# A rotary-embedding kernel: the two batches of a paired transfer lie 12 MB apart in DRAM instead of 2 MB

## Chip, cores and metric

The kernel runs on one core of a Trainium2 chip. The metric is the time of one execution in device microseconds (us), with the median over several executions.

## The reference

`x` has 16 batches of 512 positions with 1024 numbers each, read as 16 heads of 64. Each head is cut into halves `x1` and `x2`, which are rotated by tables that depend on the position alone:

```python
cos = cos[None, :, None, :]
sin = sin[None, :, None, :]
rotated = np.concatenate([x1 * cos - x2 * sin, x1 * sin + x2 * cos], axis=-1)
```

Input and output are 33.55 MB each. Every number is read once and written once, with two products and one sum on it.

## The kernel before

Batches 0, 1, 14 and 15 travel alone, as 128 partitions with 4 positions (16 KB) each. Batches 2 to 13 travel in pairs: 64 row groups of 8 positions (32 KB) from each of two batches, so that partition 2s belongs to the first batch of the pair and partition 2s + 1 to the second. A tile of `x` lands in a ring of 40 rows in on-chip memory, is worked on in place and is stored from there.

```python
singles = (0, 1, batch - 2, batch - 1)
tiles = [(b, R1 if b in singles else R2) for b in range(batch) if b in singles or b % 2 == 0]
RING = 5 * R2
...
x2 = x.rearrange("b (s r) d -> s b (r d)", r=R2)
...
def in_dram(single, pairs, t):
    b, n = tiles[t]
    return single[b] if n == R1 else pairs[:, b:b + 2, :]
...
def on_sync(sp):                       # all loads
    for t, (b, n) in enumerate(tiles):
        if b * R1 % R2 == 0 and b * R1 >= RING:
            k = (b * R1 - RING) // R2
            sp.wait_ge(sem_out[k], 16 * stores_of(k))      # ring slot free
        sp.dma_start(in_sbuf(t), in_dram(x1, x2, t)).then_inc(sem_in[t], 16)
...
ae.dma_start(in_dram(o1, o2, t), in_sbuf(t))               # the stores, from ScalarE's queue
```

Per row, GpSimd (POOL) forms the product with `sin` (58 of the 64 rows; VectorE forms it for one row of each pair tile), VectorE (DVE) the product with `cos`, and the sum is made by VectorE or, for 21 of the 64 rows, by TensorE (PE) with ScalarE (ACT) copying it back.

## Time and profile before

| | before |
|---|---|
| time, median of 3 | 161.3 us (161.3 to 161.43) |
| the profiled execution, and its span | 167.47 us, 166.1 us: slow state |
| DMA engines busy, loads + stores | 48.3% + 47.3% of 16 engines |
| POOL, DVE, PE busy | 82%, 79%, 44% |
| moved | 67.26 MB |

The span is the time from the first to the last instruction. The share of the DMA queues is the time that their packets took, against 16 engines over the whole span, so two queues that add up to nearly 100% leave hardly any moment in which an engine has nothing to move.

### The profile page before, as it was taken

What the parts mean: (1) busy time and instruction counts of PE and PEld (TensorE: products, weight loads), DVE (VectorE), ACT (ScalarE), POOL (GpSimd) and SP (SyncE); (2) the same over time, 40 slices, a digit from 0 to 9 for tenths busy, and PEclk for the clock granted to TensorE, in tenths of its full rate; (3) what the DMA queues carried; (4) which work ended last, traced back from release to release, by engine and by line L of the source; (5) the groups of instructions that cost most, each with busy time, mean ns of one, the idle gap of its engine ahead of it and who ended that gap; (6) DMA issues with size and microseconds to landing.
All of it is one profiled execution on the core that took longest, in us unless ns stands there. A gap on an engine that the chain in (4) does not pass through costs nothing.

```text
span 166.1 us, 568 instructions
## 1 busy us (share of the span) xinstructions
PE 72.6 (44%) x94; PEld 24.6 (15%) x94; DVE 130.5 (79%) x117; ACT 24.0 (14%) x26; POOL 136.6 (82%) x67
## 2 busy tenths in 40 slices
PE   6040006196629371924292909381193827800000
PEld 1020002041202011301130213020130212200000
DVE  0069997798999999999999899972999997069600
ACT  3020000204022201222022011302022022110000
POOL 5059999999999999999999799962999999069500
PEclk9999999957696975599659555955559555595555
DMA  5999999999999999999989999999999999999293
GB/s 158 427 425 458 450 391 426 462 391 418 446 489 387 444 434 403 482 363 412 466 387 482 395 403 466 395 442 426 403 478 426 387 422 458 442 395 434 107 383 142
DMA packets 3170, 67.26 MB, mean 405 GB/s; under 512 B 352, under 2 KB 608, under 8 KB 608
## 3 DMA queue, kind: packets, MB, share of 16 engines
q1 hardware_dynamic: 1728, 33.69, 48.3%
q10 hardware_dynamic: 1440, 33.56, 47.3%
q14 instruction: 2, 0.02, 0.0%
HBM read 33.69 MB, written 33.55 MB: 405 GB/s over the span
## 4 chain that ended last, share of the span: by engine, by line
DMA 52%; POOL 15%; issue 11%; DVE 8%; PE 6%; ACT 1%; SPq 1%; POOLq 0%; DVEq 0%; ACTq 0%
DMA x_sb<-in_x_dram 33%; DMA out_dram<-x_sb 19%; POOL t_sb L254 15%; PE t_ps L209 6%; DVE x_sb L301 4%; DVE t_ps L290 4%; ACT x_sb L175 1%; SPq L156 1%; SPq L159 1%; DVE t_sb L283 0%; DVEq L300 0%; POOLq L145 0%; POOLq L143 0%; ACTq L136 0%
## 5 line engine op out<-in xcount | busy, mean ns | idle before, releaser
L254 POOL TENSOR_TENSOR t_sb<-x_sb,s_sb 128x1024 f32<-128x1024 f32 x58 | 134.2, 2355 | 18.7 <-DMA x_sb<-in_x_dram 11.7
L209 PE MATMUL t_ps<-t_sb,ident 128*128 128x512 f32 x84 | 67.8, 966 | 65.3 <-POOL t_sb L254 45.1
L290 DVE TENSOR_TENSOR t_ps<-x_sb,pair_ps 128x1024 f32<-128x1024 f32 x48 | 57.9, 1222 | 8.1 <-DMA x_sb<-in_x_dram 4.8
L301 DVE TENSOR_TENSOR x_sb<-t_ps,t_sb 128x1024 f32<-128x1024 f32 x43 | 52.4, 1220 | 2.7 <-POOL t_sb L254 2.5
L209 PEld LDWEIGHTS t_ps<-t_sb,ident 128*128 128x128 f32 x84 | 22.7, 295 | 109.6 <-issue 62.1
L175 ACT ACTIVATE x_sb<-t_ps 128x1024 f32<-128x1024 f32 x21 | 21.5, 1024 | 112.0 <-PE t_ps L209 112.0
L290 DVE TENSOR_TENSOR t_ps<-x_sb,tab_ps 128x1024 f32<-128x1024 f32 x16 | 19.3, 1222 | 7.1 <-DMA x_sb<-in_x_dram 6.7
L283 DVE TENSOR_TENSOR t_sb<-x_sb,tab_ps 128x1024 f32<-128x1024 f32 x6 | 7.3, 1215 | 0.0
L261 DVE COPY tab_ps<-stage 128x128 f32<-128x128 f32 x1 | 0.3, 295 | 8.1 <-DMA stage<-in_cos_dram 8.1
L192 PE MATMUL pair_ps<-stage,pick 128*128 128x256 f32 x4 | 2.0, 664 | 5.6 <-DMA stage<-in_sin_dram 5.6
L185 PE MATMUL t_ps<-zero 128*128 128x512 bf16 x6 | 2.7, 630 | 1.3 <-DVE zero L259 1.3
L192 PEld LDWEIGHTS pair_ps<-stage,pick 128*128 128x128 f32 x4 | 1.2, 322 | 6.6 <-issue 6.4
L235 POOL TENSOR_SCALAR_AFFINE_SELECT pick<-pick 128x128 f32<-128x128 f32 x2 | 1.4, 706 | 0.1
L165 ACT ACT_TABLE_LOAD x1 | 1.3, 1283 | 0.8 <-PEq L334 0.8
L165 ACT ACTIVATE s_sb<-stage 128x128 f32<-128x128 f32 x1 | 0.3, 309 | 7.4 <-DMA stage<-in_sin_dram 7.4
L185 PEld LDWEIGHTS t_ps<-zero 128*128 128x128 bf16 x6 | 0.7, 137 | 2.4 <-DVE zero L259 1.2
L259 DVE MEMSET zero<- 128x256 uint32 x1 | 0.3, 272 | 0.9 <-PEq L334 0.9
L169 ACT ACTIVATE s_sb<-pair_ps 128x256 f32<-128x256 f32 x1 | 0.4, 384 | 1.7 <-PE pair_ps L192 1.7
L220 POOL MEMSET ident<- 128x128 f32 x1 | 0.2, 205 | 0.3 <-POOLq L334 0.3
L170 ACT ACTIVATE s_sb<-pair_ps 128x256 f32<-128x256 f32 x1 | 0.4, 377 | 0.0
L222 POOL TENSOR_SCALAR_AFFINE_SELECT ident<-ident 128x128 f32<-128x128 f32 x1 | 0.3, 297 | 0.1
L334 POOL MEMSET const-float32-0.0<- 128x1 f32 x1 | 0.1, 99 | 0.3 <-issue 0.3
(7 smaller groups left out, 1.3 us busy)
## 6 DMA issues: line engine op xcount, KB each, us to landing
x_sb<-in_x_dram SPq DMA_DIRECT2D x6, 4096.0 KB, 39.3
out_dram<-x_sb ACTq DMA_DIRECT2D x6, 4096.0 KB, 30.4
x_sb<-in_x_dram SPq DMA_DIRECT2D x4, 2048.0 KB, 24.3
out_dram<-x_sb ACTq DMA_DIRECT2D x4, 2048.0 KB, 17.6
stage<-in_cos_dram SPq DMA_DIRECT2D x1, 64.0 KB, 8.0
stage<-in_sin_dram SPq DMA_DIRECT2D x1, 64.0 KB, 7.7
```

The lines of the kernel that those rows point to most:

```text
L156: sp.dma_start(in_sbuf(t), in_dram(x1, x2, t)).then_inc(sem_in[t], 16)
L159: sp.dma_start(stage[:, i, :], table.rearrange("(s r) d -> s (r d)", r=R1)).then_inc(sem, 16)
L165: ae.activation(s1_sb[:, :, 0, :], sv, COPY, scale=-1.0)
L175: ae.activation(xs[:, k, :], t1_ps[:, u % NT1, :], COPY).then_inc(sem_a, 1)
L185: pe.matmul(t1_ps[:, k, b * BANK:(b + 1) * BANK], zero[:, 0:P], zero[:], start=True, stop=True).then_inc(sem_w, 1)
L192: pe.matmul(pair_ps[:, k].rearrange("p c r d -> p (c r d)"), pick[:, k].rearrange("q s b -> q (s b)"), stage[:].rearrange("q c f -> q (c f)"),
L209: ins = pe.matmul(t1_ps[:, u % NT1, b * BANK:(b + 1) * BANK], ident[:], t2[:, b * BANK:(b + 1) * BANK], start=False, stop=True, skip_group ...
L235: pl.affine_select(out=pick[:, k], in_=pick[:, k], compare_op=mybir.AluOpType.is_equal, fill=0.0, base=-k, pattern=[[-2, P // 2], [0, 2]], ...
L254: pl.tensor_tensor(t2_sb[:, u % NT2, :, :, :], swapped(k), over_heads(s_of(t, r)), mult).then_inc(sem_p, 1)
L283: ve.tensor_tensor(t2_sb[:, u % NT2, :, :, :], swapped(k), over_heads(v_ps), mult)
L290: ve.tensor_tensor(t1_ps[:, u % NT1, :].rearrange("p (h d) -> p h d", d=HALF), x_sb[:, k, :, :, :].rearrange("p h t d -> p (h t) d"), c_of ...
L301: ve.tensor_tensor(xs[:, k, :], t1_ps[:, u % NT1, :], t2_sb[:, u % NT2, :, :, :].rearrange("p h t d -> p (h t d)"), add,).then_inc(sem_v, 1)
```

## The change

The intent is to try whether two batches that are further apart in DRAM are read and written faster together. Pair i now joins batches 2 + i and 8 + i. As the ring slot can then no longer be worked out from the batch number, a running sum takes its place.

```diff
-    singles = (0, 1, batch - 2, batch - 1)
-    tiles = [(b, R1 if b in singles else R2) for b in range(batch) if b in singles or b % 2 == 0]
+    FAR = (batch - 4) // 2
+    tiles = [(0, R1), (1, R1)] + [(2 + i, R2) for i in range(FAR)] + [(batch - 2, R1), (batch - 1, R1)]
     NT = len(tiles)
+    first = [sum(n for _, n in tiles[:t]) for t in range(NT)]
 ...
-            return single[b] if n == R1 else pairs[:, b:b + 2, :]
+            return single[b] if n == R1 else pairs[:, b:b + FAR + 1:FAR, :]
 ...
-            k = b * R1 % RING
+            k = first[t] % RING
 ...
-            return sum(b * R1 // R2 == k for b, _ in tiles)
+            return sum(u // R2 == k for u in first)
 ...
-                if b * R1 % R2 == 0 and b * R1 >= RING:
-                    k = (b * R1 - RING) // R2
+                if first[t] % R2 == 0 and first[t] >= RING:
+                    k = (first[t] - RING) // R2
```

More of the change, by code (lines that the diff above doesn't have):

```diff
@@ L113, in in_dram @@
             b, n = tiles[t]
-            return single[b] if n == R1 else pairs[:, b:b + 2, :]
+            return single[b] if n == R1 else pairs[:, b:b + FAR + 1:FAR, :]
         def in_sbuf(t):
-            b, n = tiles[t]
-            k = b * R1 % RING
+            n = tiles[t][1]
+            k = first[t] % RING
             return x_sb[:, k:k + n].rearrange("p n h t d -> p (n h t d)")
@@ L147, in stores_of @@
         def stores_of(k):
-            return sum(b * R1 // R2 == k for b, _ in tiles)
+            return sum(u // R2 == k for u in first)
         def on_sync(sp):
-            for t, (b, n) in enumerate(tiles):
-                if b * R1 % R2 == 0 and b * R1 >= RING:
-                    k = (b * R1 - RING) // R2
+            for t in range(NT):
+                if first[t] % R2 == 0 and first[t] >= RING:
+                    k = (first[t] - RING) // R2
                     sp.wait_ge(sem_out[k], 16 * stores_of(k))
```

## The prediction

155.6 us of packets, 4.3 us for start, end and everything else, and 1.4 us between span and time make 161.3 us, to which the change adds 0. The chances, the range and the 1 to 3 us of the last sentence are the author's estimates.

> **What bounds the kernel now.** I read the page's second and third parts first, because the change touches nothing but addresses in DRAM. The question is whether the DMA engines are the bound, and if so, whether it is their own pace or the memory behind them.
>
> ```profile
> DMA  5999999999999999999989999999999999999293
> ...
> DMA packets 3170, 67.26 MB, mean 405 GB/s; under 512 B 352, under 2 KB 608, under 8 KB 608
> ## 3 DMA queue, kind: packets, MB, share of 16 engines
> q1 hardware_dynamic: 1728, 33.69, 48.3%
> q10 hardware_dynamic: 1440, 33.56, 47.3%
> ```
>
> The first line is the DMA engines' busy share in 40 slices: full from the second slice to the thirty-seventh, with one gap near the end. The last two are loads (q1) and stores (q10). Together they hold the 16 engines for 48.3 + 47.3 = 95.6% of a 166.1 us span, while POOL, the busiest compute engine, is at 82%. So the whole kernel is one stream of transfers with little slack. The windows view (busy times of each engine, then the granted clock, the DMA share and GB/s) says the same by stage:
>
> ```profile
> 10.00:55.00 45.00, 20.50 (x28) 7.08 (x27) 41.83 (x39) 5.78 (x7) 44.98 (x20) 0.85 1.01 433
> 55.00:95.00 40.00, 21.38 (x29) 6.93 (x28) 38.75 (x35) 7.17 (x7) 38.84 (x18) 0.73 1.01 427
> 95.00:120.00 25.00, 10.27 (x14) 3.69 (x14) 20.40 (x19) 4.10 (x4) 20.59 (x10) 0.57 0.98 421
> 120.00:146.00 26.00, 17.25 (x20) 5.67 (x20) 19.07 (x17) 5.12 (x5) 20.55 (x9) 0.58 1.01 430
> 146.00:157.00 11.00, 0.00 (x0) 0.00 (x0) 9.13 (x8) 0.00 (x0) 9.27 (x4) 0.62 0.76 328
> ```
>
> From 10 to 146 us the rate is 421 to 433 GB/s whether loads run alone, loads and stores are mixed, or stores prevail. Only the last stretch falls. There the chain that ended last shows why:
>
> ```profile
> 94.96 36.53 DMA x_sb<-in_x_dram
> ...
> 133.88 6.96 POOL t_sb L254 x3
> 140.84 5.82 issue
> ...
> 149.00 6.97 POOL t_sb L254 x3
> ...
> 156.07 1.22 DVE x_sb L301
> ```
>
> The last two loads are issued at 95 us and sit behind the other transfers. POOL stands still for 5.82 us until the last single batch lands at 146.6, needs about 9.3 us for its four rows, VectorE adds the last row at 156.07, and the last store ends the span at 166. The end is thus the landing of the last load plus a fixed tail, and that landing is set by how fast the engines work off what is queued.
>
> The trace's packet records give that pace. A 32 KB packet, which is one row of one batch of a pair, has a median of 1213 ns on the load queue and the same on the store queue; a 16 KB packet of a single batch has 611 ns on both. Per engine there are 48 packets of 32 KB and 32 of 16 KB in each direction: 2 x (48 x 1.213 + 32 x 0.611) = 155.6 us. An unprofiled run takes 161.3 us; taking off the 1.4 us by which the profiled run's time (167.47) exceeds its span (166.1), about 159.9 us are left. So 155.6 of 159.9 us is packets at their usual length, and 4.3 us are the start, the end and everything else.
>
> [...]32768 bytes in 1213 ns on 16 engines is 432 GB/s, and stretches reach 433.[...] This kernel's pairs already are 2 MiB apart[...]: their packets run at 27.0 GB/s an engine, and those of the single batches, with no second batch in them, at 16384 / 611 = 26.8.[...]
>
> **The change part by part.** It removes and adds no instruction: the instruction order of the two built programs is the same on every engine, with line numbers shifted by two. The ring slots are the same: the first row of each tile was four times its batch number and is now a running sum, which gives 0, 4, 8, 16, 24, 32, 40, 48, 56, 60 in both. The waits of the loads on the three early store semaphores, and the number of stores that each counts, are the same. So the cost on SP, ACT, POOL, PE and DVE is 0.
>
> What moves are addresses. Each pair load and store still names 64 rows of two batches with one unbroken run of 32 KB each; only the step between the batches grows from 2 MB to 12 MB. The packets keep their count (768 loads, 768 stores of 32 KB), their size[...]. Second, while pair t is stored, the load running a few tiles ahead is now at another distance in the tensor: a pair's two streams move on by 2 MB instead of 4 MB. The singles at the start and end are untouched, so the tail after the last landing keeps its length.
>
> The only term is then the packet length. Each engine carries 96 pair packets (48 in, 48 out), so every 10 ns on each of them is 0.96 us on the time. Upwards, 2% (3.2 us) needs 34 ns more on every pair packet, or 2.8%. Downwards, the means are 1233 ns (loads) and 1225 ns (stores) against the median of 1213, so a perfect memory would give back 48 x 20 + 48 x 12 ns, about 1.5 us or 0.9%. [...]in the records one chain of packets, evidently one engine, has 27 of the 96 packets that are more than 100 ns over the usual length, in part at a steady 2 to 3 us.[...] I expect a change of 0, between -0.4 and +0.8 us.
>
> **The rivals.**
> First, the wide step hurts[...]. For it: some packets do run long, in bursts around 72 to 75 and 92 to 95 us. Against it: those bursts are at ends of loads, at most a few hundred ns each; from the 10th to nearly the 90th percentile a 32 KB load packet takes 1213 to 1228 ns[...].[...]
>
> Second, the wide step helps, as its author must have hoped: two batches 2 MB apart were in each other's way, and now are not. Against it is the flat 1213 ns. At its best it gives the 1.5 us worked out above, so 159.8 us. A gain of 2% would need packets faster than the median that both queues and both sizes share.
>
> Third, nothing in the memory changes but one engine's lag does. In this profile the last load's 16 completions are spread from 138.7 to 146.6 us, so one late engine holds POOL by several us, and the profiled run is 3.8% longer than the unprofiled ones. If the new addresses changed the lag, profiles would differ by some us while the unprofiled times stay put. I take the unprofiled time as the measure, where the before runs lie within 0.13 us.
>
> **Range and chances.** The first rival gets 3%, the second at its full size 5% (which still counts as within 2%), the rest is no change with some scatter. So I predict 161.3 us, from 160.6 to 162.2 in 8 of 10 cases; faster by over 2%: 0.01, within 2%: 0.96, slower by over 2%: 0.03.
>
> **What would show it.** Right: the same packet and byte counts on q1 and q10, 32 KB packets with a median of 1213 ns within a few ns on both queues, 420 to 435 GB/s from 10 to 146 us, and the same instruction durations (POOL 2355 ns, DVE 1220 ns). Wrong by the first rival: q1's or q10's share of the engines grows at the same bytes, and the middle stretches fall under 415 GB/s. Wrong by the second: medians below 1213 ns, or bursts of long packets gone with the unprofiled time down by 1 us or more. What I can't read from one profile is how far the unprofiled run is free of the late engine; if that lag is in the memory and in every run, a gain or loss of 1 to 3 us could come from there.

## More of the kernel before

Executions come in two states. Most agree within some 0.3% ("fast"); a few take some per cent longer ("slow").

Note the state: the profile at hand for the prediction was of a slow execution, while the time to be predicted is that of fast ones.

## The result

The changed kernel takes 161.34 us (median of 6, 161.28 to 161.51), the kernel before 161.34 us (median of 6, 161.30 to 161.53). The ratio is 0.9999, with a 95% interval from 0.9987 to 1.0012. Ratios in this document are the mean time of one kernel's fast executions over that of the other's of the same rounds, so they are not quite the ratio of the medians. The result is correct.

The page of the changed kernel's profile, a fast execution this time, first with the busy share of the DMA engines in 40 slices and the two queues:

```profile
DMA  5999999999999999999999999999999999999996
...
DMA packets 3170, 67.26 MB, mean 421 GB/s; under 512 B 352, under 2 KB 608, under 8 KB 608
...
q1 hardware_dynamic: 1728, 33.69, 49.8%
q10 hardware_dynamic: 1440, 33.56, 48.8%
```

The packets and bytes are as before. The share is 98.6%, that is 157.7 us of packets in a span of 159.9 us, and the gap near the end of the earlier profile is gone. By stage (the windows view; the columns are the stretch, its length, busy time of PE, PE's weight loads, DVE, ACT and POOL, the granted clock, the DMA share and GB/s):

```profile
10.00:55.00 45.00, 18.99 (x27) 6.05 (x26) 41.81 (x39) 5.78 (x7) 45.00 (x20) 0.85 1.01 433
55.00:95.00 40.00, 23.12 (x29) 7.59 (x28) 39.18 (x36) 7.22 (x8) 40.00 (x18) 0.66 1.00 432
95.00:120.00 25.00, 12.00 (x17) 4.11 (x18) 22.97 (x21) 4.04 (x4) 22.53 (x11) 0.70 1.00 432
120.00:146.00 26.00, 11.67 (x17) 3.87 (x15) 20.83 (x19) 5.12 (x5) 22.38 (x11) 0.76 1.00 432
146.00:157.00 11.00, 0.00 (x0) 0.00 (x0) 4.07 (x4) 0.00 (x0) 3.82 (x2) 0.50 0.97 417
```

The rate is 432 or 433 GB/s from 10 to 146 us, and 417 even in the stretch that held 328 in the slow profile. The chain that ended last closes like this (start, length, what):

```profile
73.29 38.12 DMA x_sb<-in_x_dram
...
136.94 3.58 issue
...
142.86 6.97 POOL t_sb L256 x3
...
149.92 1.22 DVE x_sb L303
```

POOL waits 3.58 us for the last load where it had waited 5.82, and the last row is done at 151.1 us instead of 157.3. Read against the profile before, this looks like a gain of 6 us. The times say that there is none. The first thing to settle was thus whether those 6 us belong to the change or to the state of the execution.

### The profile page after: what moved, and what is told of

It is laid out like the page before. It is cut to its first block, busy times and chain, and to the rows that moved or that the text cites. A ratio compares the mean times of both kernels' runs of the same rounds, so it can differ in the third digit from the quotient of the medians.

```text
span 159.9 us, 568 instructions
## 1 busy us (share of the span) xinstructions
PE 69.4 (43%) x94; PEld 23.1 (14%) x94; DVE 130.2 (81%) x117; ACT 23.9 (15%) x26; POOL 136.4 (85%) x67
## 3 DMA queue, kind: packets, MB, share of 16 engines
q1 hardware_dynamic: 1728, 33.69, 49.8%
## 4 chain that ended last, share of the span: by engine, by line
DMA 52%; POOL 17%; issue 9%; DVE 8%; PE 6%; ACT 1%; SPq 1%; POOLq 0%; DVEq 0%; ACTq 0%
DMA x_sb<-in_x_dram 35%; POOL t_sb L256 17%; DMA out_dram<-x_sb 17%; PE t_ps L211 6%; DVE x_sb L303 4%; DVE t_ps L292 4%; ACT x_sb L177 1%; SPq L158 1%; SPq L161 1%; DVE t_sb L285 1%; DVEq L302 0%; POOLq L145 0%; POOLq L147 0%; DVEq L147 0%; ACTq L138 0%
## 5 line engine op out<-in xcount | busy, mean ns | idle before, releaser
L211 PE MATMUL t_ps<-t_sb,ident 128*128 128x512 f32 x84 | 64.6, 919 | 63.3 <-POOL t_sb L256 40.4
L292 DVE TENSOR_TENSOR t_ps<-x_sb,pair_ps 128x1024 f32<-128x1024 f32 x48 | 57.8, 1222 | 5.1 <-ACT x_sb L177 3.4
L303 DVE TENSOR_TENSOR x_sb<-t_ps,t_sb 128x1024 f32<-128x1024 f32 x43 | 52.5, 1220 | 2.7 <-POOL t_sb L256 2.5
L211 PEld LDWEIGHTS t_ps<-t_sb,ident 128*128 128x128 f32 x84 | 21.2, 278 | 106.5 <-DVE t_ps L292 58.0
L292 DVE TENSOR_TENSOR t_ps<-x_sb,tab_ps 128x1024 f32<-128x1024 f32 x16 | 19.3, 1222 | 4.5 <-DMA x_sb<-in_x_dram 4.4
L285 DVE TENSOR_TENSOR t_sb<-x_sb,tab_ps 128x1024 f32<-128x1024 f32 x6 | 7.3, 1215 | 0.0
```

What stands on the lines that cost most here:

```text
L211: ins = pe.matmul(t1_ps[:, u % NT1, b * BANK:(b + 1) * BANK], ident[:], t2[:, b * BANK:(b + 1) * BANK], start=False, stop=True, skip_group ...
L285: ve.tensor_tensor(t2_sb[:, u % NT2, :, :, :], swapped(k), over_heads(v_ps), mult)
L292: ve.tensor_tensor(t1_ps[:, u % NT1, :].rearrange("p (h d) -> p h d", d=HALF), x_sb[:, k, :, :, :].rearrange("p h t d -> p (h t) d"), c_of ...
L303: ve.tensor_tensor(xs[:, k, :], t1_ps[:, u % NT1, :], t2_sb[:, u % NT2, :, :, :].rearrange("p h t d -> p (h t d)"), add,).then_inc(sem_v, 1)
```

## The experiments

All ran on the same kind of chip with three rounds. Three theories were in play. A: the DMA engines' own pace sets the time, and the addresses of the pairs do not matter. B: the long packets of one engine in the first profile come from the 2 MB neighbours, and the change cures them. C: far loads and far stores have opposite effects that cancel. D to H came with the controls.

### e1_before_again: the kernel before, unchanged

No edit.

> The kernel before, unchanged, for a profile in the fast state. Theory A (the DMA engines' own pace is the bound and addresses do not matter): 161.3 us, ratio 1.000, and if the profile is fast, a span near 159.9 us with 32 KB packets at a median of 1213 ns and the last load's completions within some 2 us of each other, as in the profile after. Theory B (the late engine of the first profile comes from the 2 MB neighbours in memory, and the far pairs cured it): a span over 163 us again, with the last load's completions spread by over 5 us.

It took 161.48 us (median of 4, 161.31 to 161.76), ratio 1.0014 (0.9999 to 1.0029) to other executions of itself. Its profile was fast, with a span of 159.9 us. Its queues, then two stretches of it in the windows view:

```profile
q1 hardware_dynamic: 1728, 33.69, 49.8%
q10 hardware_dynamic: 1440, 33.56, 48.7%
```

```profile
120.00:146.00 26.00, 13.61 (x17) 4.26 (x15) 20.81 (x19) 5.12 (x5) 22.37 (x11) 0.63 1.01 434
146.00:157.00 11.00, 0.00 (x0) 0.00 (x0) 4.14 (x4) 0.00 (x0) 3.89 (x2) 0.50 0.97 417
```

The unchanged kernel shows what the changed one does: 417 GB/s in the last full stretch, and the same shares within 0.1%. In the trace's completion records the last load's 16 engines finish between 139.6 and 140.6 us here and between 138.9 and 140.5 in the changed kernel; in the slow profile it was 138.7 to 146.6. The 32 KB packets have a median of 1213 ns on both queues; their means are 1222 (loads) and 1214 ns (stores), against 1220 and 1215 in the changed kernel. Theory B falls: the late engine is a mark of the slow execution, not of the addresses. The state also turned up elsewhere: one of four executions of the run with far stores took 165.53 us, and one of seven of the kernel before, in the last set of rounds, 167.29. Slow executions were too few to tell whether the addresses change how often the state comes: two of the kernel before, one with far stores, none among the six of the changed kernel.

### e2_far_loads and e3_far_stores: one half of the change each

```diff
+        def near(single, pairs, t):
+            b, n = tiles[t]
+            return single[b] if n == R1 else pairs[:, 2 * b - 2:2 * b, :]
 # e2_far_loads: the stores take neighbours
-                    ae.dma_start(in_dram(o1, o2, t), in_sbuf(t))...
+                    ae.dma_start(near(o1, o2, t), in_sbuf(t))...
 # e3_far_stores: the loads take neighbours
-                sp.dma_start(in_sbuf(t), in_dram(x1, x2, t))...
+                sp.dma_start(in_sbuf(t), near(x1, x2, t))...
```

> Pairs 12 MB apart in the loads alone; the stores go to neighbours, so the result is wrong on purpose (batches exchanged). Theory A: 161.3 us, ratio within 0.998 to 1.002. Theory C (far loads help and far stores hurt, or the reverse, and the two cancelled in the change): at least 1 us away from 161.3, and the run with far stores alone as far on the other side.

> Pairs 12 MB apart in the stores alone; wrong result on purpose. Theory A: 161.3 us, ratio within 0.998 to 1.002. Theory C: at least 1 us away from 161.3, opposite to the run with far loads alone.

Far loads alone: 161.47 us, ratio 1.0014 (0.9997 to 1.0031). Far stores alone: 161.63 us over all four executions, ratio of the fast three 1.0014 (0.9998 to 1.0031). Both were wrong in the result. The unchanged kernel had 1.0014 in the same rounds, so all three stand at the same place and 0.14% is the scatter of such a comparison. Packet medians are 1213 ns in both. Theory C falls: neither half does anything by itself.

### e7_dma_only_near and e8_dma_only_far: the transfers without any compute

```diff
         on_sync(nc.sync)
-        on_scalar(nc.scalar)
-        on_gpsimd(nc.gpsimd)
-        on_tensor(nc.tensor)
-        on_vector(nc.vector)
+        copy_out(nc.scalar)    # for each tile: wait for its load, store it
```

The first is made from the kernel before, the second from the changed one.

> The kernel before without any compute: the same loads, ring and waits, each tile stored as soon as it has landed, wrong result on purpose. Theory A: packets of 155.6 us per engine plus start and end, so 158 to 161 us, with only the first load's wait and the last store's tail left. If compute set the end: below 150 us, which the packet lengths forbid unless packets get shorter.

> The changed kernel without any compute, for the disputed cost by itself. Theory A: equal to the near one of the same kind within 0.3 us. If the compute's waits hid a gain or a loss of the far addresses in the change: over 1 us apart from it.

The near one took 161.17 us, ratio 0.9992 (0.9978 to 1.0007) to the full kernel before, the far one 161.36, ratio 1.0000 (0.9985 to 1.0015). The page of the near one, its span and the DMA row, and then two stretches in the windows view, where only POOL's column is left ahead of the clock, the DMA share and GB/s:

```profile
span 159.7 us, 39 instructions
...
DMA  5999999999999999999999999999999999999997
```

```profile
120.00:146.00 26.00, 0.00 (x0) 1.00 1.01 434
146.00:157.00 11.00, 0.00 (x0) 1.00 1.00 427
```

Removing all the arithmetic, 568 instructions down to 39, moves the span from 159.9 to 159.7 us. The far one, in the same two stretches:

```profile
120.00:146.00 26.00, 0.00 (x0) 1.00 1.01 433
146.00:157.00 11.00, 0.00 (x0) 1.00 1.00 427
```

The expected range for the near one ended at 161 us, so the median missed it by 0.17 us: I had allowed too little for the start and the end. With the compute gone, 32 KB load packets have a mean of 1213 ns at near and 1214 ns at far addresses. The two ratios' intervals overlap, and the medians lie 0.19 us apart, within the 0.3 us expected. The disputed cost measured by itself is nil at this resolution.

### e6_half_load: fewer bytes, same compute

```diff
+                src, dst = in_dram(x1, x2, t), in_sbuf(t)
+                if t == NT - 3:
+                    src, dst = src[:, :, 0:R1 * dim], dst[:, 0:R1 * dim]
-                sp.dma_start(in_sbuf(t), in_dram(x1, x2, t))...
+                sp.dma_start(dst, src)...
```

> The last pair load brings only half of each row: 2.1 MB less of 67.24 MB, packets of 16 KB in that load, all compute and stores as before, wrong result on purpose. Theory A: 128 packets shorter by 602 ns over 16 engines is 4.8 us less, so 156.5 us. If compute on POOL or its waits were the bound: less than 1.5 us saved.

It took 156.56 us (156.46 to 156.80), ratio 0.9706 (0.9690 to 0.9722), with this line on its page:

```profile
DMA packets 3170, 65.16 MB, mean 420 GB/s; under 512 B 352, under 2 KB 608, under 8 KB 608
```

The saving is 161.35 - 156.56 = 4.8 us for 2.1 MB, with every arithmetic instruction in place: the amount worked out from packet lengths beforehand. Compute is thus not the bound. This run alone doesn't tell the bytes from "the last load's landing plus a fixed tail", as the last load landed earlier by nearly as much (135.8 us against 140.5); the run without compute does, as its last load landed at 151.8 us and its span is the same. Bytes over the engines' pace are the bound.

### e5_hot_loads: one row for everybody

```diff
-                sp.dma_start(in_sbuf(t), in_dram(x1, x2, t))...
+                row = x2[0:1, b:b + 1, :].broadcast_to([P // 2, 2, R2 * dim]) if n == R2 else x1[b]
+                sp.dma_start(in_sbuf(t), row)...
```

> Each pair load reads one and the same 32 KB row for all its 128 partitions (same packets and bytes, stores as before, wrong result on purpose). The other extreme of locality. Theory A in its strong form: 161.3 us, 1213 ns a packet. Theory D (the place in memory can matter): load packets away from 1213 ns by over 5% and the time by over 2 us; slower if the one row is a hot spot, faster if a nearer row serves reads quicker.

It took 161.48 us, ratio 1.0017 (0.9993 to 1.0041), with load packets at a median of 1213 ns and a mean of 1217. Even when all 128 partitions of a tile come from one 32 KB row, so that the six pair loads read six such rows in all, the engines go neither faster nor slower. This is the strongest sign that no gain was to be had here from better placed reads.

### e4_wide_loads: all 16 batches in each load

```diff
+        xw = x.rearrange("b (s r) d -> b s (r d)", r=R2)
-                sp.dma_start(in_sbuf(t), in_dram(x1, x2, t))...
+                i = t - 2
+                wide = xw[:, 8 * i:8 * i + 8, :] if n == R2 else x1[b]
+                sp.dma_start(in_sbuf(t), wide)...
```

> Each pair load takes eight 32 KB rows from each of all 16 batches, so neighbouring groups of eight partitions are 2 MB apart, many streams at once instead of two; the stores are as before, wrong result on purpose. A positive control for memory addresses. Theory A in its strong form (no address pattern of 32 KB rows matters here): 161.3 us, 1213 ns a packet. Theory D ([...]two streams are too few to show it): load packets longer than 1300 ns and a time over 164 us.

It took 193.38 to 204.76 us, too scattered for a ratio. The stretch from 12 to 20 us, in which loads run alone (those of a single batch until about 13 us, then those of the first pair), in the windows view, first of this run and then of the unchanged kernel:

```profile
12.00:20.00 8.00, 0.00 (x0) 0.00 (x0) 8.00 (x7) 0.00 (x0) 8.00 (x4) 1.00 1.08 250
```

```profile
12.00:20.00 8.00, 0.00 (x0) 0.00 (x0) 7.94 (x7) 0.00 (x0) 8.00 (x4) 1.00 1.00 432
```

The engines are as busy but move 250 instead of 432 GB/s: in that stretch a 32 KB packet takes 2528 ns in the median, not 1213. From 14 to 20 us, where only the pair load is left, it is 191 against 431 GB/s. So a load pattern can slow this kernel, and the profile shows it at once in GB/s and packet length. The strong form of theory A does not hold for this load. Whether the wide pattern's place in memory is the reason, as theory D says, was asked by four more runs.

### e9_wide_skew, e12_wide_skew4k, e10_wide_1mb and e11_inner: what about the wide loads is slow

```diff
+        xrows = x.rearrange("b (s r) d -> (b s) (r d)", r=R2)
 # 16 groups of 8 rows, `step` apart
+                    wide = xrows[8 * i:8 * i + 16 * 65 - 57, :]
+                    wide = bass.AP(tensor=wide.tensor, offset=wide.offset, ap=[[step, 16], [R2 * dim, 8], [1, R2 * dim]])
 # e9_wide_skew:     step = 65 * R2 * dim          (2 MB + 32 KB)
 # e12_wide_skew4k:  step = 64 * R2 * dim + dim    (2 MB + 4 KB)
 # e10_wide_1mb:     step = 32 * R2 * dim          (1 MB; the slice shortened to match)
 # e11_inner: 16 rows by 8 batches, the 2 MB step inside
+        xq = x.rearrange("b (s r) d -> s b (r d)", r=R2)
+                    inner = xq[16 * (i // 2):16 * (i // 2) + 16, 8 * (i % 2):8 * (i % 2) + 8, :]
```

> As the wide loads of all 16 batches (which took 193 to 205 us), but each batch's eight rows begin one 32 KB row later than the one before's, so the step is 2 MB + 32 KB; wrong result on purpose. Theory E ([...]an offset of this size resolves it): 161 to 165 us, load packets back at 1213 ns. Theory F (the number of far-apart streams is what costs, whatever the pitch): 190 us or more.

> The same with a step of 2 MB + 4 KB[...]; wrong result on purpose. Theory E: 161 to 165 us. Theory F: 190 us or more.

> The wide loads with a step of 1 MB instead of 2 MB between the 16 groups of eight rows (8 batches' extent); wrong result on purpose. Theory E[...]: between 161 and 190 us, so less than the 2 MB step. Theory F: 190 us or more, as the streams are as many.

> Each pair load takes 16 rows of 8 batches with the 2 MB step in the inner dimension, as the pairs have it: neighbouring partitions are 2 MB apart[...]; wrong result on purpose. Theory G (only what different engines read at the same moment counts[...]): 161 to 163 us, 1213 ns a load packet. Rival H (far-apart batches within one transfer cost, whichever dimension has the step, and two of them were merely too few to show it): over 170 us.

| run | step between the 16 groups | ratio of fast executions | GB/s from 12 to 20 us |
|---|---|---|---|
| e4_wide_loads | 2 MB | none (193.38 us the fastest) | 250 |
| e9_wide_skew | 2 MB + 32 KB | 1.201 (1.190 to 1.212) | 242 |
| e12_wide_skew4k | 2 MB + 4 KB | 1.212 (1.199 to 1.224) | 242 |
| e10_wide_1mb | 1 MB | 1.223 (1.216 to 1.230) | 242 |
| e11_inner | 32 KB (2 MB in the inner dimension) | 1.194 (1.184 to 1.204) | 244 |

The last one in the windows view:

```profile
12.00:20.00 8.00, 0.00 (x0) 0.00 (x0) 7.96 (x7) 0.00 (x0) 8.00 (x4) 1.00 1.07 244
```

Theory E, that an offset from the 2 MB step restores the pace, falls: neither offset helps, and half the pitch helps nothing. That half the pitch should cost less, between 161 and 190 us, rested on no run. Theory G, that only what different engines read at once counts, is not borne out: with the step put inside, the cost is the same. This run weighs little against it, though, as its 161 to 163 us rested on which engine meets which batch, which was not shown. Theory F (many far-apart streams cost, whatever the pitch) and rival H (many batches in one transfer cost, whichever dimension) both passed. But that nothing in the addresses changes the size of the effect points to something that these five runs share and that I had not thought of when I designed them: their DRAM side is 16 groups of 8 rows, while the pairs, and the hot row, have an outer dimension of 64. The measured packet medians of the five runs, 2528 to 2555 ns, are about twice the 1213 ns of the pairs. Why it is twice is not shown, and the trace does not name the engine of a packet. The run that would tell is a 16 by 8 load over nearly contiguous rows, and it was not made. It stays open whether shape or many streams costs here, and theory D with it. What is shown does not hang on it: two streams, 2 or 12 MB apart, cost nothing.

## Why the prediction was right

The number, 161.3 us, is the time measured before; what was predicted is that nothing is added to it, and why.

- **The DMA engines bound the kernel: right, and shown.** Without arithmetic the time stays (161.17 us), with 2.1 MB less it drops by 4.8 us.
- **The end is the last load's landing plus a fixed tail: this step was wrong for fast executions**, though it moved no number. It was read from the slow profile, where the queues had run nearly dry before the last store. In the fast profiles of both kernels the engines are 97% busy from 146 to 157 us, and the kernel that has no compute tail at all ends at 159.7 us against 159.9. The last store is issued at 151.2 us, but its packets begin only at about 153.7, when the engines are done with the store before; in the slow profile one packet was in flight when it was issued at 157.4 us, and its own began at 158.2. In the fast state the end is set by the packets queued, not by the last row.
- **155.6 of 159.9 us are packets at their usual length: right.** The fast profile of the unchanged kernel has 49.8 + 48.7 = 98.5% of 159.9, or 157.5 us in packets: 1.9 us over the usual lengths and 2.4 us of idling, nearly all before the first packet at 1.8 us and after the last at 159.5. Together they make up the 4.3 us.
- **Three readings of the slow profile were loose, without effect on the forecast.** No stretch of its table holds loads alone, since the first store is issued at 20.7 us; the stretch from 12 to 20 us, shown with the wide loads, does, at 432 GB/s. The bursts at 72 to 75 us reach 2260 ns, so up to 1047 ns over the usual length and not "a few hundred". The chain said to hold 27 of the 96 long packets holds 22 to 24 when the packets are linked anew by their times, at intervals of 2.0 to 2.8 us for long stretches.
- **No instruction, wait, packet or byte changes, only addresses: right.** The pages agree in all counts.
- **Packet length does not change: right.** The median is 1213 ns before and after, on both queues; the means differ by about 2 ns.
- **First rival, the wide step hurts: it fell for two batches**, with loads and stores separately and together, with compute and without.
- **Second rival, the wide step helps: it fell, and its best case was too large.** The 1.5 us came from means of the slow profile. With the means of the fast one, 1222 and 1214 ns, the same sum is 48 x 9 + 48 x 1 ns, about 0.5 us. The hot row shows that even this was not to be had from placement.
- **Third rival, one engine's lag: right in what it warned of.** The spans of the first two profiles differ by 6 us while the times agree. But profiling alone does not cause the lag: later profiled executions of the changed and the unchanged kernel took 161.28 and 161.34 us. What does cause it is not shown.

## What to carry to other kernels

Before moving data to better addresses, look at the packet lengths. Here nearly all 32 KB packets took 1213 ns on loads and stores alike, at nearly the same rate as the 16 KB ones (27.0 and 26.8 GB/s an engine), and a friendlier place in memory had nothing to give. One common length alone doesn't say so: in the wide loads, nearly all 32 KB packets from 14 to 20 us took 2498 to 2560 ns, evenly slow. All of this holds for one core working alone; no run has a second one beside it. Check the state of a profile before reading its tail: one slow execution showed a gap and a late engine that fast executions of the same kernel do not have, and a wait of POOL of 5.82 us where a fast one has 3.60. The last load's 16 completions were spread over 7.9 us in the slow one, against 1.0 and 1.6 in the fast profiles of the two kernels. The granted clock does not tell the state: 0.711 in the slow profile, 0.65 to 0.80 in fast executions of the same two kernels, and 1.0 without compute at the same time. And vary a control's shape and its addresses separately, or it will show that something matters without telling what.
